# The tail of a two-layer backbone: wide products for output tiles 4 to 6, the last tile finished half by half

## Chip, cores and metric

The kernel runs on one core of a Trainium2 chip. The metric is device time of one execution in microseconds (us), median of several runs. The engines of the core are named as in the profile: PE (TensorE, products), DVE (VectorE), ACT (ScalarE), POOL (GpSimd) and SP (SyncE, which issues the transfers here). Each engine works through its own instructions strictly in the order in which they were placed, and waits for the others by semaphores.

## What is computed

A backbone of two layers over 1024 latent tokens and 256 context tokens with 1024 features: windowed attention, then a bidirectional state-space mixer (SSD), each with a gated residual, and a final normalisation. What matters here is the end of the second layer and the last line:

```python
def rms_normalize(x):
    xf = x.astype(jnp.float32)
    return (xf * lax.rsqrt(jnp.mean(xf * xf, axis=-1, keepdims=True) + EPS)).astype(x.dtype)

def back(y_f, y_b, xs, z):                      # end of the SSD mixer
    ...
    u = rms_normalize(u.reshape(bsz, n, SSD_GROUPS, SSD_WIDTH // SSD_GROUPS))
    return (u.reshape(bsz, n, SSD_WIDTH) * norm_w) @ w_out      # 2048 -> 1024

    h = h + gate[:, None] * y
return rms_normalize(h) * final_norm_w
```

So for each token: a product of 2048 features with `w_out` gives 1024 outputs, a gate and the residual `h` follow, and the token is scaled by the root of the mean of its 1024 squares and by a weight per output.

## The kernel before

**Layout.** Outputs lie on partitions: the 1024 outputs are eight tiles m = 0 to 7 of 128, tokens run along the free axis in two blocks, 0 to 511 and 512 to 1023. An fp32 product is made of three: features and weights are split into a high part in a rounded format (`oH`, `wh`) and the rest (`oL`, `wl`), and `mm3` (L223 to L225) sums high x high, low x high and high x low in one accumulator. For one output tile that is 16 feature tiles x 3 products.

**Stages of `ssd_out`.** Sweeps of products (L1571, 512 tokens wide, four output tiles at once, beside the last state-space work) finish all eight tiles of the first 512 tokens and tiles 0 to 3 of the second 512. Gates for these are the DVE operations of L1577. Then comes the tail, which the change rewrites:

- The first 512 tokens: `rstd_c` turns the sums of squares (`prev["acc"]`) into 1/root. PE sums over partitions (L344), ACT takes the root (L352), DVE the reciprocal (L353) and a diagonal matrix with it (L355), PE spreads that over all partitions (L357), ACT copies the result to SBUF (L359). `tail` then scales each of the eight tiles on DVE (L1479, one operation for weight and 1/root) and SP stores it (L1482). These tiles lie in the buffers named `uH` and `uL` in the profile.
- Tiles 4 to 7 of the second 512 tokens: each tile has two accumulators of 256 tokens in the two buffers `pj2`. For each of two steps (e = 0, 1: eight feature tiles each) it loads 512 KB of weights (L216, `wr`), ACT rounds them (L209, `wh`), DVE takes the rest (L211, `wl`), and PE runs 24 products for the first 256 tokens and 24 for the second (L223 to L225, 256 wide). There are two buffers each of `wr`, `wh` and `wl`. Then come the gates of both halves (L1611), and `final` adds their squares (ACT L1467 or L1470, POOL or DVE L1471).
- The second 512 tokens, after all products: `rstd_c` for each half of 256, and `tail` for pairs of tiles, six on DVE, tiles 3 and 7 (`TAILP`) with the 1/root on POOL (L1476) and the weight on ACT (L1477). One store per pair and half; the tiles lie in buffers named `xn`.

**What sets the order.** The code gives a program order; a scheduler then places the instructions of each engine by its own estimates of when they can start, keeping all dependencies. So the order on an engine can differ from the code, and it is fixed when the kernel is built.

Of the kernel before, what the change touches and what calls it, by code (L numbers as in the profile page):

```python
# [17 lines left out]
P = 128  # L18
D = 1024
KT = D // P  # L20
LAT = 1024
# [21 lines left out]
    pj=1, S=2, pt=2, pv=1,  # L43
# [8 lines left out]
PARTS = 8  # L52
SLACK = (0, 0, 0)
QC = 5
TAILP = (3, 7)
N512, N256 = 0.229, 0.120
FRONT = 4 * 48 * N512 + 3 * 24 * N256 + 8 * 24 * N256
OUT = 4 * 30 * 3 * N512
# [46 lines left out]
class Kernel:  # L105
# [1327 lines left out]
    def ssd_out(self, p, spare, sp, sc, post):  # L1433


        nc, t, a = self.nc, self.t, self.a
        ps = self.psA
        BUFS.update(oraw=4)
        fw = t(self.cp, [P, KT], F32, "fw")
        nc.sync.dma_start(fw, a["final_w"])  # L1440
        h, pair, prev = {}, {}, {}

        def weights(m, k0, k1):
            w = []
            for e in range(2):
                lo, hi = max(k0, 8 * e), min(k1, 8 * e + 8)
                if lo < hi:
                    wh, wl = self.load_w(a["w_so"][m, e][:, (lo - 8 * e) * P : (hi - 8 * e) * P], hi - lo)
                    w += [(wh[:, x], wl[:, x]) for x in range(hi - lo)]
            return w  # L1450

        def residual(m, s, n):
            i = s // 512
            if i == 0:
                if m % 4 == 0:
                    self.h4 = t(self.up, [P, 4, n], F32, ("uH2", "uL2")[m // 4])
                h[m] = self.h4[:, m % 4]
            else:
                if m % 2 == 0:
                    pair[m] = self.h4 = t(*spare[m // 2])  # L1460
                h[m] = self.h4[:, m % 2]
            nc.sync.dma_start(h[m], self.h_d[m][i][:, s - 512 * i : s - 512 * i + n])

        def square(m, s, n, hm, first, dve):
            if first:
                self.acc = t(*{0: (sp, [P, n], F32, "xn2"), 512: (sp, [P, n], F32, "bn2"), 768: (sc, [P, n], F32, "xs")}[s])
                nc.scalar.activation(self.acc, hm, AF.Square)  # L1467
            else:
                sq = t(sp, [P, 512], F32, "bn4")[:, :n]
                nc.scalar.activation(sq, hm, AF.Square)  # L1470
                (nc.vector if dve else nc.gpsimd).tensor_tensor(self.acc, self.acc, sq, op=ALU.add)  # L1471

        def tail(s, n, h, r, k, m0):
            for m in range(m0, m0 + k):
                if k > 1 and m in TAILP:
                    nc.gpsimd.tensor_tensor(h[m], h[m], r, op=ALU.mult)  # L1476
                    nc.scalar.activation(h[m], h[m], AF.Copy, scale=fw[:, m : m + 1])  # L1477
                else:
                    nc.vector.scalar_tensor_tensor(h[m], in0=h[m], scalar=fw[:, m : m + 1], in1=r, op0=ALU.mult, op1=ALU.mult)  # L1479
            src = h[m0] if k == 1 else pair[m0][:, :, s - 512 : s - 512 + n]  # L1480
            dst = a["out"][m0 * P : (m0 + k) * P, s : s + n]
            nc.sync.dma_start(dst if k == 1 else dst.rearrange("(a p) n -> p a n", p=P), src)  # L1482
# [58 lines left out]
        for n, (i, mg, qs) in enumerate(sweeps):  # L1541
            if n == 3:
                alloc(1, 1)
            pj = [t(ps, [P, 2, 512], F32, "pj2") for _ in range(2)]
# [5 lines left out]
            for q in qs:  # L1550
                w = ws[j]
# [4 lines left out]
                for z in range(2):  # L1556
                    k = 2 * q + z
# [26 lines left out]
        post.flush()  # L1584

        self.ptag = "psX"
        acc, hs = {}, {512: {}, 768: {}}

        def final(m, s):
            h[m] = hs[s][m] = pair[m - m % 2][:, m % 2, s - 512 : s - 256]  # L1590
            self.acc = acc.get(s)
            square(m, s, 256, h[m], m == 0, m == KT - 1)
            acc[s] = self.acc

        for m in range(4):
            for s in (512, 768):
                final(m, s)
        r = self.rstd_c(p, prev["acc"], 512, D, rout=(sc, [P, 512], F32, "y2"), dout=(sp, [P, 512], F32, "bn4"))
        for m in range(KT):
            tail(0, 512, prev["h"], r, 1, m)  # L1600
        for m in range(4, KT):
            residual(m, 512, 512)
            full = h[m]
            pj = {s: t(ps, [P, 512], F32, "pj2")[:, :256] for s in (512, 768)}
            for e in range(2):
                w = weights(m, 8 * e, 8 * e + 8)
                for s in (512, 768):
                    self.mm3(pj[s], [(*w[k], self.oH[e][:, k, s - 512 : s - 256], self.oL[e][:, k, s - 512 : s - 256]) for k in range(8)], e == 0, e == 1)
            for s in (512, 768):
                h[m] = full[:, s - 512 : s - 256]  # L1610
                nc.vector.scalar_tensor_tensor(h[m], in0=pj[s], scalar=self.mod[1][:, 16 + m, 0:1], in1=h[m], op0=ALU.mult, op1=ALU.add)  # L1611
                final(m, s)
        r = {s: self.rstd_c(p, acc[s], 256, D, rout=(sc, [P, 256], F32, x), dout=(sp, [P, 512], F32, "bn4")) for s, x in ((512, "y2"), (768, "hx"))}
        for m in range(0, KT, 2):
            for s in (512, 768):
                tail(s, 256, hs[s], r[s], 2, m)

    def dump_split(self, name, h, l, i, n, s):
        nc = self.nc
# [97 lines left out]
```

## Time and profile before

| | |
|---|---|
| median of 3 runs | 1819.51 us (1817.31 to 1822.76) |
| profiled execution, its own time | 1818.37 us |
| its span, first to last instruction | 1816.6 us |
| PE busy | 1749.0 us, 96% |
| DVE, ACT, POOL busy | 64%, 48%, 45% |
| mean granted PE clock | 0.99 |
| last product of the tail ends | about 1800.9 us |

Rows of a chain or a timeline give start, length, engine, what is written (`<-` what is read), line, and a count where several are merged. Buffer numbers are left out, so `pj` is any product accumulator, `psX` a small accumulator, `bn` a scratch tile. A bracket at the end of a row is the idle time of the engine before it, and what ended it.

### The profile page before, as it was taken

What the parts mean: (1) busy time and instruction counts of PE and PEld (TensorE: products, weight loads), DVE (VectorE), ACT (ScalarE), POOL (GpSimd) and SP (SyncE); (2) the same over time, 40 slices, a digit from 0 to 9 for tenths busy, and PEclk for the clock granted to TensorE, in tenths of its full rate; (3) what the DMA queues carried; (4) which work ended last, traced back from release to release, by engine and by line L of the source; (5) the groups of instructions that cost most, each with busy time, mean ns of one, the idle gap of its engine ahead of it and who ended that gap; (6) DMA issues with size and microseconds to landing.
All of it is one profiled execution on the core that took longest, in us unless ns stands there. A gap on an engine that the chain in (4) does not pass through costs nothing.

```text
span 1816.6 us, 29129 instructions
## 1 busy us (share of the span) xinstructions
PE 1749.0 (96%) x10379; PEld 1500.2 (83%) x10379; DVE 1166.0 (64%) x2125; ACT 869.9 (48%) x1895; POOL 811.1 (45%) x1074
## 2 busy tenths in 40 slices
PE   6999998999999899999999999999999999999997
PEld 3797767788889687778898898989889898988886
DVE  3563536786787766675766748567675857766643
ACT  3521235677788766352444434344353434544522
POOL 2441127554456465303454544646454454644311
PEclk9999999999999999999999999999999999999998
DMA  8768865543345445311322323323332322655542
GB/s 296 285 156 255 261 192 138 119 116 99 99 117 132 118 133 195 112 42 52 86 68 79 93 69 88 82 71 79 78 93 78 82 79 74 188 163 179 163 137 70
DMA packets 209393, 227.89 MB, mean 125 GB/s; under 512 B 16096, under 2 KB 149088, under 8 KB 208224
## 3 DMA queue, kind: packets, MB, share of 16 engines
q1 hardware_dynamic: 175184, 207.38, 38.1%
q0 software_dynamic: 34064, 18.65, 5.6%
q8 instruction: 82, 1.34, 0.3%
q14 instruction: 63, 0.52, 0.1%
HBM read 191.14 MB, written 35.13 MB: 125 GB/s over the span
## 4 chain that ended last, share of the span: by engine, by line
PE 83%; DVE 5%; ACT 4%; DMA 4%; issue 3%; POOL 0%; SPq 0%; DVEq 0%; ACTq 0%; POOLq 0%
PE pj L1152 17%; PE pj L1177 10%; PE pj L1571 7%; PE pj L223 6%; PE pj L225 6%; PE pj L224 6%; PE psD L1143 3%; PE pt L694 3%; PE psX L1311 2%; PE pv L701 2%; PE psD L1236 2%; PE pv L700 2%; PE S L669 2%; PE psX L1285 1%; PE S L670 1%
## 5 line engine op out<-in xcount | busy, mean ns | idle before, releaser
L223 PE MATMUL pj<-uH,wh 128*128 128x256 f32 (+1 forms) x652 | 233.5, 358 | 8.1 <-DVE rope_b L532 2.3
L224 PE MATMUL pj<-uL,wh 128*128 128x256 f32 (+1 forms) x652 | 220.1, 338 | 0.0
L225 PE MATMUL pj<-uH,wl 128*128 128x256 f32 (+1 forms) x652 | 220.1, 338 | 0.0
L211 POOL TENSOR_TENSOR wl<-wr,wh 128x512 fp32r<-128x512 f32 x92 | 121.7, 1326 | 97.4 <-ACT wh L209 96.9
L1152 PE MATMUL pj<-uH,wh 128*128 128x512 f32 x480 | 161.4, 410 | 2.0 <-ACT xn L1088 1.2
L1152 PE MATMUL pj<-uH,wl 128*128 128x512 f32 x480 | 158.5, 403 | 0.0
L1152 PE MATMUL pj<-uL,wh 128*128 128x512 f32 x480 | 157.3, 402 | 0.0
L699 DVE TENSOR_TENSOR pl<-pt,ph 128x512 fp32r<-128x512 f32 x168 | 114.2, 687 | 61.3 <-ACT ph L698 60.4
L223 PEld LDWEIGHTS pj<-uH,wh 128*128 128x128 f32 x652 | 124.7, 191 | 34.9 <-issue 8.6
L1177 PE MATMUL pj<-wh,uH 128*128 128x256 f32 x512 | 148.0, 289 | 3.1 <-ACT xn L1088 3.0
L1177 PE MATMUL pj<-wl,uH 128*128 128x256 f32 x512 | 150.7, 294 | 0.0
L1213 POOL TENSOR_TENSOR xw<-xn,dtdec 128x256 f32<-128x256 f32 x144 | 92.9, 649 | 127.1 <-PE psD L1236 108.5
L1177 PE MATMUL pj<-wh,uL 128*128 128x256 f32 x512 | 149.5, 292 | 0.0
L1342 ACT ACTIVATE uT<-psX,nw 128x128 f32<-128x128 f32 x128 | 46.7, 365 | 193.2 <-PE psX L1341 193.1
L225 PEld LDWEIGHTS pj<-uH,wl 128*128 128x128 f32 x652 | 124.4, 191 | 14.8 <-issue 1.7
L673 DVE CUSTOM_DVE_ANT_0 sm<-S,mask,nsink 128x640 f32<-128x640 f32 (+2 forms) x160 | 118.7, 772 | 26.5 <-PE S L670 14.5
L224 PEld LDWEIGHTS pj<-uL,wh 128*128 128x128 f32 x652 | 124.9, 192 | 11.5 <-issue 2.8
L209 ACT CAST wh<-wr 128x512 fp32r<-128x512 f32 (+1 forms) x132 | 84.8, 645 | 102.5 <-PE pj L224 78.7
L698 ACT CAST ph<-pt 128x512 fp32r<-128x512 f32 x168 | 97.5, 585 | 64.5 <-PE pt L694 58.9
L675 ACT ACTIVATE sm<-sm,nm 128x640 f32<-128x640 f32 (+2 forms) x160 | 118.5, 742 | 12.6 <-DVE nm L673 12.3
L1152 PEld LDWEIGHTS pj<-uL,wh 128*128 128x128 f32 x480 | 90.1, 188 | 19.0
L1152 PEld LDWEIGHTS pj<-uH,wh 128*128 128x128 f32 x480 | 89.1, 188 | 19.6 <-ACT bn L1088 2.0
(383 smaller groups left out, 4999.8 us busy)
## 6 DMA issues: line engine op xcount, KB each, us to landing
fd<-acs SPq DMA_DIRECT2D x64, 256.0 KB, 5.0
bd<-acs SPq DMA_DIRECT2D x64, 256.0 KB, 5.2
wr<-w_x SPq DMA_DIRECT2D x31, 512.0 KB, 3.8
wr<-w_sk SPq DMA_DIRECT2D x24, 512.0 KB, 4.0
wr<-wg SPq DMA_DIRECT2D x44, 256.0 KB, 4.6
qs<-q POOLq DMA_DIRECT2D x40, 256.0 KB, 3.9
wr<-wo SPq DMA_DIRECT2D x40, 256.0 KB, 2.7
wada<-w_ad SPq DMA_DIRECT2D x8, 1024.0 KB, 6.4
```

The lines of the kernel that those rows point to most:

```text
L211: (eng or nc.vector).tensor_tensor(l, raw, h, op=ALU.subtract)
L223: self.nc.tensor.matmul(ps, lh, rh, start=first and i == 0, stop=False)
L224: self.nc.tensor.matmul(ps, lh, rl, start=False, stop=False)
L225: self.nc.tensor.matmul(ps, ll, rh, start=False, stop=last and i == n - 1)
L673: nc.vector.tensor_tensor_reduce(out=sm[:, :W], in0=Sv, in1=self.mask[:, m0 : m0 + W], scale=-SCALE, scalar=self.nsink[:, 4 * j + r : 4 * ...
L675: nc.scalar.activation(sm[:, :W], sm[:, :W], AF.Exp, bias=nm[:, r : r + 1], scale=-1.0, accum_out=sums[:, r : r + 1])
L698: nc.scalar.copy(ph, ptf)
L699: nc.vector.tensor_sub(pl, ptf, ph)
L1152: nc.tensor.matmul(raw[:, 512 * i : 512 * i + 512], l[:, k, :], r[i][:, k, :], start=k + y == 0, stop=k == KT - 1 and y == 2)
L1177: nc.tensor.matmul(pj[:, c], l, r[:, k, :], start=c % 2 + q + k + y == 0, stop=c % 2 == 1 and q == 1 and k == 3 and y == 2)
L1213: nc.gpsimd.tensor_tensor(xw, X(st, c).rearrange("p (r h) -> p r h", r=R), self.dtdec[:, c, hd(d, g)].unsqueeze(2).broadcast_to([P, R, HP] ...
L1571: nc.tensor.matmul(banks[x], l[:, z, sl], r, start=k == 2 * qs[0] and y == 0, stop=k == 2 * qs[-1] + 1 and y == 2)
```

## The change

1. Tiles 4 to 6 of the second 512 tokens use one accumulator of 512 tokens and 512-wide products: 48 products a tile instead of 96.
2. Weights are asked for one step ahead in the code.
3. The last tile keeps two halves of 256 tokens with an accumulator each. Each half runs all its products, then its gate, its square and its own `finish`: row sums, root, reciprocal, diagonal, spread, scaling of all eight tiles, stores.
4. The weight of the last line is multiplied in ahead (`square_w` for tiles 0 to 6, one line in the loop for tile 7, on ACT), so that `finish` only multiplies by 1/root: tiles in pairs, three pairs on DVE, which reads the factor from PSUM (`pr`), tiles 2 and 3 on POOL, which reads the copy in SBUF (`r`).
5. In `tail`, which now serves the first 512 tokens alone, odd tiles go to POOL (factor) and ACT (weight), even ones stay on DVE. The calls stand between the steps of products instead of ahead of them.
6. Squares of the second 512 tokens are summed 512 wide on POOL, in a buffer `cT`; the last tile's squares are added by PE as a second product of the row sum.

```diff
-TAILP = (3, 7)
...
         def tail(s, n, h, r, k, m0):
             for m in range(m0, m0 + k):
-                if k > 1 and m in TAILP:
+                if m % 2:
                     nc.gpsimd.tensor_tensor(h[m], h[m], r, op=ALU.mult)
                     nc.scalar.activation(h[m], h[m], AF.Copy, scale=fw[:, m : m + 1])
                 else:
...
+        acc = t(sp, [P, LAT], F32, "cT")[:, :512]
+
+        def square_w(m):
+            if m == 0:
+                nc.scalar.activation(acc, h[m], AF.Square)
+            else:
+                sq = t(sp, [P, 512], F32, "bn4")
+                nc.scalar.activation(sq, h[m], AF.Square)
+                nc.gpsimd.tensor_tensor(acc, acc, sq, op=ALU.add)
+            nc.scalar.activation(h[m], h[m], AF.Copy, scale=fw[:, m : m + 1])
+
+        def gated(m, pj, sl):
+            nc.vector.scalar_tensor_tensor(h[m][:, sl], in0=pj, scalar=self.mod[1][:, 16 + m, 0:1], in1=h[m][:, sl], op0=ALU.mult, op1=ALU.add)
+
+        def finish(i, sq):
+            pn = t(ps, [P, 512], F32, "psX")
+            lo = 256 * i
+            for b in range(2):
+                for x, y in enumerate((acc[:, lo:], sq)):
+                    nc.tensor.matmul(pn[:, b : b + 1], y[:, b * P : (b + 1) * P], self.ones[:, 0:1], start=x == 0, stop=x == 1)
+            rc = t(p, [P, 4], F32, "rc", 2)[:, :2]
+            nc.scalar.activation(rc, pn[:, :2], AF.Sqrt, bias=self.eps, scale=1.0 / D)
+            nc.vector.reciprocal(rc, rc)
+            dg = t(sp, [P, 512], F32, "bn4")[:, :256].rearrange("p (b n) -> p b n", b=2)
+            nc.vector.tensor_tensor(dg, self.ident.unsqueeze(1).broadcast_to([P, 2, P]), rc.unsqueeze(2).broadcast_to([P, 2, P]), op=ALU.mult)
+            pr = t(ps, [P, 512], F32, "psX")[:, :256]
+            nc.tensor.matmul(pr, self.ones, dg.rearrange("p b n -> p (b n)"), start=True, stop=True)
+            r = t(sc, [P, 256], F32, ("y2", "hx")[i])
+            nc.scalar.copy(r, pr)
+            for m in (0, 2, 4, 6):
+                v = pair[m][:, :, lo : lo + 256]
+                eng, x = (nc.gpsimd, r) if m == 2 else (nc.vector, pr)
+                eng.tensor_tensor(v, v, x.unsqueeze(1).broadcast_to([P, 2, 256]), op=ALU.mult)
+                nc.sync.dma_start(a["out"][m * P : (m + 2) * P, 512 + lo : 768 + lo].rearrange("(a p) n -> p a n", p=P), v)
 
         for m in range(4):
-            for s in (512, 768):
-                final(m, s)
+            square_w(m)
+        w = weights(4, 0, 8)
         r = self.rstd_c(p, prev["acc"], 512, D, rout=(sc, [P, 512], F32, "y2"), dout=(sp, [P, 512], F32, "bn4"))
-        for m in range(KT):
-            tail(0, 512, prev["h"], r, 1, m)
-        for m in range(4, KT):
+        for m in range(4, KT - 1):
             residual(m, 512, 512)
...
-            pj = {s: t(ps, [P, 512], F32, "pj2")[:, :256] for s in (512, 768)}
+            pj = t(ps, [P, 512], F32, "pj2")
             for e in range(2):
...
+                cur, w = w, weights(m + e, 8 - 8 * e, 16 - 8 * e)
+                self.mm3(pj, [(*cur[k], self.oH[e][:, k, :], self.oL[e][:, k, :]) for k in range(8)], e == 0, e == 1)
+                tail(0, 512, prev["h"], r, 1, 2 * m - 8 + e)
+            gated(m, pj, slice(0, 512))
+            square_w(m)
+        m = KT - 1
+        residual(m, 512, 512)
+        ws7 = [w, weights(m, 8, 16)]
+        for x in (6, 7):
+            tail(0, 512, prev["h"], r, 1, x)
+        for i in range(2):
+            sl = slice(256 * i, 256 * i + 256)
+            pj = t(ps, [P, 512], F32, "pj2")[:, :256]
+            for e in range(2):
+                self.mm3(pj, [(*ws7[e][k], self.oH[e][:, k, sl], self.oL[e][:, k, sl]) for k in range(8)], e == 0, e == 1)
+            gated(m, pj, sl)
+            sq = t(sp, [P, 512], F32, "bn4")[:, :256]
+            nc.scalar.activation(sq, h[m][:, sl], AF.Square)
+            nc.scalar.activation(h[m][:, sl], h[m][:, sl], AF.Copy, scale=fw[:, m : m + 1])
+            finish(i, sq)
```

Up to the start of tile 4 the order of PE, DVE, POOL and SP is the same in both kernels, and ACT's up to the last squares of tiles 0 to 3. Line numbers in the changed kernel are one lower up to the tail (L1478 is the former L1479), and the gate is L1598.

On DVE, around the gate of tile 4 (the one that writes `xn` from an accumulator `pj`), this stands in a row before; `wl` is the rest of the weights of one step, and `uH`, `uL` are the scaled tiles of the first 512 tokens:

```order
L211 TENSOR_TENSOR wl_18684<-wr_18680,wh_18682 128x1024
L1479 SCALAR_TENSOR_TENSOR uH_3616_17227<-uH_3616_17227,fw_17207,y_3856_18539 128x512 x4
L1479 SCALAR_TENSOR_TENSOR uL_3720_17728<-uL_3720_17728,fw_17207,y_3856_18539 128x512 x4
L1611 SCALAR_TENSOR_TENSOR xn_3857_18557<-pj_3858_18559,mod_6_75,xn_3857_18557 128x256
L1611 SCALAR_TENSOR_TENSOR xn_3857_18557<-pj_3859_18560,mod_6_75,xn_3857_18557 128x256
L211 TENSOR_TENSOR wl_18738<-wr_18734,wh_18736 128x1024
```

And there now:

```order
L210 TENSOR_TENSOR wl_18579<-wr_18575,wh_18577 128x1024
L1478 SCALAR_TENSOR_TENSOR uH_3616_17227<-uH_3616_17227,fw_17207,y_3855_18538 128x512 x2
L1478 SCALAR_TENSOR_TENSOR uL_3720_17728<-uL_3720_17728,fw_17207,y_3855_18538 128x512 x2
L1598 SCALAR_TENSOR_TENSOR xn_3856_18540<-pj_3857_18542,mod_6_75,xn_3856_18540 128x512
L210 TENSOR_TENSOR wl_18619<-wr_18615,wh_18617 128x1024
```

Four scalings instead of eight stand ahead of the gate, and one gate of 512 takes the place of two of 256. The other four scalings are now POOL and ACT instructions.

On PE, the end of the last tile now; `psX` is the row sum of half 0, `cT` the squares of tiles 0 to 6, `bn` those of tile 7, and `pj_3892` the accumulator of half 1:

```order
L223 MATMUL pj_3892_18845<-uL_3805_18199,wh_18761 128x256
L1605 MATMUL psX_18823<-ones_68,bn_3886_18820 128x1
L1605 MATMUL psX_18823<-ones_68,cT_18505 128x1
L1605 MATMUL psX_18823<-ones_68,bn_3886_18820 128x1
L224 MATMUL pj_3892_18845<-uH_3804_18198,wl_18763 128x256
```

Before, all products of both halves stand ahead of the first row sum:

```order
L224 MATMUL pj_3890_18918<-uL_3805_18199,wh_18975 128x256
L225 MATMUL pj_3890_18918<-uH_3804_18198,wl_18977 128x256
L344 MATMUL psX_19035<-ones_68,bn_3844_18505 128x1 x2
L357 MATMUL psX_19043<-bn_3901_19041,ones_68 128x256
L344 MATMUL psX_19047<-ones_68,xs_18507 128x1 x2
```

Half 0's row sums now stand seven products ahead of the end of half 1, whose last 34 products all come after half 0's last.

On DVE after the last gate, where `psX_18833` is the spread factor of half 0 and `psX_18908` that of half 1:

```order
L1598 SCALAR_TENSOR_TENSOR xn_3873_18685<-pj_3892_18845,mod_6_75,xn_3873_18685 128x256
L1618 TENSOR_TENSOR xn_3808_18202<-xn_3808_18202,psX_18833 128x2x256
L1618 TENSOR_TENSOR xn_3856_18540<-xn_3856_18540,psX_18833 128x2x256
L1618 TENSOR_TENSOR xn_3873_18685<-xn_3873_18685,psX_18833 128x2x256
L1608 RECIPROCAL rc_18903<-rc_18903 128x2
L1610 TENSOR_TENSOR bn_3896_18906<-ident_63,rc_18903 128x256
L1618 TENSOR_TENSOR xn_3808_18202<-xn_3808_18202,psX_18908 128x2x256
```

Six narrow scalings per half have become three wide multiplies, and half 1's reciprocal stands behind those of half 0.

On SP, loads of weights (`wr`) and stores of the first 512 tokens (`out`), now:

```order
L215 DMA wr_18647<-w_so 128x1024
L1481 DMA out<-uH_3616_17227 128x512 x3
L1481 DMA out<-uL_3720_17728 128x512 x2
L1481 DMA out<-uH_3616_17227 128x512
L1481 DMA out<-uL_3720_17728 128x512
L215 DMA wr_18688<-w_so 128x1024
L1481 DMA out<-uL_3720_17728 128x512
L215 DMA wr_18720<-w_so 128x1024
```

The load for tile 6's second step (`wr_18688`) stands behind seven of the eight stores, three of which wait for POOL and ACT; before, it stood behind all eight, which waited for DVE alone.

More of the change, by code (lines that the diff above doesn't have):

```diff
@@ L1586, in ssd_out @@
         self.ptag = "psX"
[L1587 to L1593, printed above, removed]
+        acc = t(sp, [P, LAT], F32, "cT")[:, :512]
[7 more added lines that the diff above has]
+            nc.scalar.activation(h[m], h[m], AF.Copy, scale=fw[:, m : m + 1])
@@ L1605, in ssd_out @@
             for e in range(2):
[L1606 to L1616, printed above, removed]
+                cur, w = w, weights(m + e, 8 - 8 * e, 16 - 8 * e)
+                self.mm3(pj, [(*cur[k], self.oH[e][:, k, :], self.oL[e][:, k, :]) for k in range(8)], e == 0, e == 1)
+                tail(0, 512, prev["h"], r, 1, 2 * m - 8 + e)
```

1 line of the change is left out of this document (removed).

## Prediction

> **What bounds the kernel now.** The page first: TensorE (PE) is busy almost throughout, so only a place where PE waits, or where nothing is left for it, can give time.
>
> ```profile
> span 1816.6 us, 29129 instructions
> PE 1749.0 (96%) x10379; PEld 1500.2 (83%) x10379; DVE 1166.0 (64%) x2125; ACT 869.9 (48%) x1895; POOL 811.1 (45%) x1074
> ```
>
> The change touches only what comes after the last sweep of products, from about 1750 us on. So the second view is the busy time in five stretches of that tail (columns: stretch, its length, busy us of PE, weight loads, DVE, ACT and POOL, then granted clock, DMA share, GB/s).
>
> ```profile
> 1762.50:1764.70 2.20, 0.28 (x3) 0.12 (x2) 2.20 (x5) 1.19 (x2) 0.00 (x0) 1.00 1.03 393
> 1764.70:1768.40 3.70, 3.70 (x19) 3.70 (x20) 1.29 (x2) 0.67 (x2) 2.15 (x2) 0.54 0.97 329
> 1768.40:1774.00 5.60, 5.60 (x49) 5.60 (x49) 0.86 (x1) 1.05 (x1) 0.00 (x0) 1.00 0.12 50
> ...
> 1800.90:1816.60 15.70, 2.54 (x13) 1.66 (x11) 8.80 (x18) 3.67 (x9) 3.17 (x4) 0.66 0.39 134
> ```
>
> PE is lost in three places: a hole at 1762.7, 3.7 us at a granted clock of 0.54 after it, and 15.7 us at the end with hardly a product. Third view, the chain of waits across the hole (start, length, what), and PE's own row at its end:
>
> ```profile
> 1728.56 11.04 PE pj L1571 x48
> ...
> 1750.09 0.36 PE pj L223
> ...
> 1757.16 0.88 PE psX L357 x2
> 1758.06 0.60 ACT y L359
> 1758.68 2.74 DVE uH L1479 x4
> 1761.42 1.35 DVE uL L1479 x3
> ...
> 1763.99 0.49 DVE xn L1611
> ...
> 1764.61 0.36 PE pj L223
> ...
> 1768.50 0.12 PE pj L223
> ```
>
> ```profile
> 1764.61 0.36 PE L223 MATMUL pj<-uH,wh 128*128 128x256 f32 x1 [1.92 <-DVE xn L1611]
> ```
>
> DVE scales eight finished tiles of the first 512 tokens (L1479) in one run; the gate of output tile 4 (L1611) stands behind them, and tile 5 can't start, since both its accumulators are still held by tile 4. Fourth, the chain from the last product to the end, POOL's part of the first half's scaling, the first two store issues of the second half, and the bytes per second in 40 slices of 0.325 us from 1804:
>
> ```profile
> 1800.90 0.35 PE psX L344 x4
> ...
> 1801.28 0.27 ACT rc L352
> ...
> 1801.57 0.18 DVE rc L353
> ...
> 1801.77 0.44 DVE bn L355
> ...
> 1802.35 0.68 PE psX L357 x2
> ...
> 1803.46 2.70 DVE xn L1479 x4
> ...
> 1807.49 1.21 PE psX L357 x2
> ...
> 1808.73 0.38 ACT hx L359
> ...
> 1811.04 1.58 DVE xn L1479 x4
> ```
>
> ```profile
> 1803.50 1.58 POOL L1476 TENSOR_TENSOR xn<-xn,y 128x256 f32<-128x256 f32 x2 [11.25 <-ACT y L359]
> ```
>
> ```profile
> 1811.07 0.89 SPq L1482 DMA_DIRECT2D out<-xn  x2
> ```
>
> ```profile
> GB/s 0 0 0 0 0 0 0 280 331 347 321 356 328 359 331 353 221 0 0 0 0 0 0 0 148 328 359 315 372 318 359 347 350 315 16 0 0 0 0 0
> ```
>
> Both 256-token halves are finished one behind the other on DVE, after all products.
>
> **The sum, part by part.** Prices come from these groups (mean ns after the bar), besides the rows above:
>
> ```profile
> L1286 DVE TENSOR_TENSOR fd<-fd,psX 128x512 f32<-128x512 f32 x64 | 43.7, 683 | 25.6 <-ACT fd L1272 13.5 <-PE psX L1282 10.3 <-PE psX L1341 1.3
> L1471 POOL TENSOR_TENSOR xn<-xn,bn 128x512 f32<-128x512 f32 x7 | 11.1, 1589 | 9.4 <-ACT bn L1470 8.9
> L291 ACT ACTIVATE uH<-uL,mod 128x512 fp32r<-128x512 f32 x12 | 8.7, 723 | 10.3 <-DVE uL L290 10.2
> L211 DVE TENSOR_TENSOR wl<-wr,wh 128x1024 fp32r<-128x1024 f32 x8 | 9.8, 1222 | 18.3 <-ACT wh L209 18.3
> L209 ACT CAST wh<-wr 128x1024 fp32r<-128x1024 f32 x8 | 8.4, 1046 | 23.8 <-PE pj L224 16.3 <-issue 4.4 <-PE pj L1571 3.1
> wr<-w_so SPq DMA_DIRECT2D x7, 512.0 KB, 3.6
> ```
>
> 1. Wide products in tiles 4 to 6. A tile now takes 96 products of 0.12 us, 11.52; afterwards 48 wide ones, and the sweep row has 48 in 11.04. Three tiles: 3 x 0.48 = 1.44 us gained, all on PE's path.
>
> 2. The hole. A tile now holds one accumulator, so tile 5 starts in the other without tile 4's gate. DVE scales four tiles instead of eight ahead of that gate, and POOL and ACT the other four. The 1.92 us go. What is late next? The weights of tile 5's second step: their low part stands on DVE behind the gate. Tile 4 now ends near 1750.1 + 11.04 + 0.88 = 1762.0; four scalings from 1758.68 take 2.74 alone, and beside POOL up to 2.70/1.58 times that (the two rows of four at the end; POOL worked beside the first from 1803.50 to 1805.08), 4.7, to 1763.4. Gate and low part (0.75 + 1.22, estimates from the gate's half of 0.49 and L211) end near 1765.5; the second step wants them at 1762.0 + 5.52 + 0.46 = 1768.0. Slack 2.5 us, cost nothing.
>
> 3. The slow clock. 3.70 us at 0.54 are 3.70 x 0.46 = 1.70 us of lost products; it follows the hole and should go with it.
>
> [...]
>
> 4. Weights a step ahead. Both kernels have two buffers of each part, so the cast for step s+1 starts when PE has left step s-1, one step (5.52 us) ahead; cast and low part need 1.05 + 1.22 = 2.3. Nothing gained, nothing lost while ACT's other new work fits: per tile two casts (2.1), a square and a weight multiply (about 0.72 each, L291), in tile 4 four more multiplies (2.9): at most 6.5 of 11.04. On SP the load for tile 6's second step now stands behind seven stores, three of which wait for POOL and ACT: POOL's four multiplies by L1471's 1.59 run to about 1765.1, so the load lands before 1770 (3.6 us); it is wanted at 1773.1. Nothing.
>
> 5. The finish. Let E be the end of the last product. PE now takes half 0's row sums in seven products before E (7 x 0.12 = 0.84). From the rows above: root 0.27, reciprocal 0.18, diagonal 0.44 with gaps of 0.02 to 0.14 end at E + 0.23; spread 0.68, copy 0.38 (DVE's multiply waits for that copy) to E + 1.3; then three multiplies on DVE of 128x2x256, with the scale read from PSUM. No row shows this shape. Lower bound and value taken 0.683 (L1286: the same size, with a broadcast operand in PSUM); upper bound 1.35, two narrow L1479 as they ran beside POOL (2 x 2.70/4). To E + 3.4. Half 1's gate, square and sums are done by then; its reciprocal and diagonal stand behind those multiplies: E + 4.2, spread 1.21 (as after the long idle now; 0.68 at best), copy: E + 5.8. The first store follows a multiply later; SP then waits for POOL's multiply of tiles 2 and 3 (1.5 taken, a little under the two narrow ones' 1.58, since it is one instruction) and issues the last three from about E + 7.3. In the trace data starts 0.9 us after the issue at 1811.07 (slice 24, 1811.9), and four stores take ten slices, 0.8 each; the last slice ends at 1815.1, 1.5 before the end of the span. So E + 7.3 + 0.9 + 2.3 + 1.5 = E + 12.0, against 15.7 now (1800.90 to 1816.6): 3.7 gained. Bounds: 0.68 for the spread gives 4.2; 1.35 for the multiplies costs 2.0 for half 0 and about as much for half 1, and nothing of the 3.7 remains.
>
> [...]
>
> Sum: 1.44 + 1.92 + 1.70 + 3.7 = 8.8, less 0.35 for the row sums that now stand between products (the row at 1800.90): 8.4 us. The profiled execution took 1818.37 (1816.6 and 1.8 around it), 1.1 under the median 1819.51, to which I apply it: 1811.1. POOL's wider sums of squares (1.59 each) lie beside products: three from about 1752, before its first multiply can start at 1758.7, then one per tile.
>
> **Rivals.** Bound of "no change": 0.3%, 5.5 us, about what a measurement of this kernel can tell.
>
> 1. As summed: 1811.1; its own range 1808 (spread 0.68 and a low run, as 1817.31 is 2.2 under its median) to 1813.5.
>
> 2. The finish gains nothing: the new multiplies take 1.35. For it: the slow first four L1479 beside POOL. Against it: the PSUM operand of L1286 at 0.683 over 64 instances. 1811.1 + 4.0 = 1815.1, "no change".
>
> 3. POOL holds DVE in the middle. If scalings and POOL's multiplies exclude each other fully, DVE's fourth ends at 1758.7 + 4 x 0.69 + 3 x 1.59 = 1766.2, and the low part, past the gate and POOL's fourth, at about 1769.2 instead of 1768.0: a hole of 1.2, and 1.7 more if the clock falls again. 1811.1 + 2.9 = 1814.0. Against it: four L1479 beside two POOL multiplies took 2.70, less than 1.58 + 1.58. [...]
>
> 4. The slow clock belongs to the burst of stores (DMA share 0.97 to 1.03 in both rows), not to the hole. The same eight stores remain. 1811.1 + 1.7 = 1812.8.
>
> 5. Slower: the weight casts come late. If ACT has over 5.52 - 2.3 = 3.2 us of other work in front of each cast, every step waits for its weights: seven further steps x 2.4 = 16.8, less 8.4: 1827.9. Only tile 4 has so much ACT work, most of it in its first step, before the next cast is possible.
>
> **How the numbers follow.** Chances: 0.60, 0.14, 0.12, 0.09, 0.05 in that order. Faster by over 0.3% (under 1814.0): 1 but for a high run (0.58), 4 (0.09), half of 3 (0.06), a part of 2 (0.05): 0.78. Within 0.3%: the rest of 1, 2 and 3: 0.17. Slower: 5, 0.05. The range runs from 1807.0 (all lower bounds and a low run) to 1815.5, just past rival 2.
>
> **What would show it.** Right: tiles 4 to 7 of products without a gap from 1750.1 to about 1796.2 with the clock at 1.00; the scaling of the first 512 tokens ends on DVE before 1764; three DVE multiplies near 0.69 us each per half; about 12 us from the last product to the end. Wrong: a PE row waiting for the low part (wl) or the cast in tile 5 or 6 (rivals 3, 5); a clock near 0.5 without a hole (4); the multiplies above 1 us (2). The part before 1750 us should not move; if it does by more than 2 us, the sum is wrong for a reason I do not see.

## The result and the profile after

The changed kernel took 1805.28 us (median of 6 runs, 1804.25 to 1809.08), the kernel before 1817.06 beside it (6 runs, 1814.91 to 1822.76): ratio 0.9935, interval [0.9918, 0.9952], a gain of 11.8 us. The forecast was 1811.1 with a range from 1807.0. Two later loads of the same two kernels gave ratios of 0.9952 [0.9940, 0.9963] and 0.9956 [0.9944, 0.9968], gains of 8.7 and 8.0 us; over all runs the medians are 1809.08 (17 runs) and 1817.26 (66 runs), 8.2 us apart. So the change is worth about 8.2 us, close to the 8.4 of the sum; what the first comparison shows beyond that comes from the part of the kernel that the change does not touch, as shown below.

The page of after (span, busy time, granted clock in 40 slices):

```profile
span 1802.2 us, 28825 instructions
...
PE 1741.2 (97%) x10243; PEld 1488.7 (83%) x10243; DVE 1162.7 (65%) x2110; ACT 875.4 (49%) x1897; POOL 815.5 (45%) x1070
...
PEclk9999999999999999999999999999999999999998
```

The span is 14.4 us shorter. I cut it at the first of the four gates that end the last sweep (L1577 before, L1576 after: 1748.53 and 1742.35 us); what follows is called the tail. The tail went from 68.08 to 59.87 us, 8.2 shorter. The other 6.2 us lie ahead of it, where both kernels have the same instructions in the same order.

First the tail. Busy time from its first product to its last, and after it (columns as in the prediction):

```profile
1743.90:1790.40 46.50, 46.45 (x250) 39.75 (x250) 21.51 (x21) 19.29 (x28) 16.25 (x10) 1.00 0.31 102
...
1790.40:1802.20 11.80, 2.81 (x12) 1.93 (x12) 4.74 (x10) 1.74 (x5) 2.54 (x2) 0.61 0.52 178
```

PE is busy 46.45 of 46.50 us at a granted clock of 1.00; the hole and the 0.54 behind it are gone. What PE waits for in the tail (in all, times, longest) names neither a low part (wl) nor a gate. This view counts idle time only; a short delay between overlapping products does not show in it (point 2 below has one).

```profile
PE psX L1612 <- DVE bn L1610: 2.3, 2, 2.1
PE pj L222 <- ACT cT L1590: 0.2, 1, 0.2
```

The chain at the end (start, length, what):

```profile
1788.85 0.57 PE psX L1605 x6
...
1790.02 0.42 DVE bn L1610
...
1790.44 0.44 DVE xn L1598
...
1791.38 0.29 ACT y L1614
...
1791.70 1.88 DVE xn L1618 x3
1793.58 0.09 DVE rc L1608
...
1793.76 0.44 DVE bn L1610
...
1794.33 1.21 PE psX L1612 x2
...
1795.56 0.38 ACT hx L1614
...
1795.97 0.69 DVE xn L1618
```

The last product ends at 1790.35, just ahead of half 1's gate (L1598), and the span at 1802.22: 11.9 us, where before had 15.7.

Now the part ahead of the tail. Three stretches of it in before, in after, and in after loaded once more (e2_after below); the column behind the last bracket is the granted clock:

```profile
255.00:355.00 100.00, 88.45 (x444) 71.34 (x443) 66.28 (x182) 58.05 (x158) 62.74 (x90) 0.93 0.56 136
...
600.00:630.00 30.00, 24.48 (x128) 18.61 (x127) 21.66 (x47) 18.75 (x42) 10.07 (x16) 1.00 0.46 122
...
740.00:840.00 100.00, 93.21 (x495) 76.40 (x494) 66.40 (x92) 45.02 (x79) 17.64 (x23) 0.98 0.22 66
```

```profile
255.00:355.00 100.00, 88.31 (x479) 71.21 (x478) 71.69 (x193) 63.48 (x171) 66.04 (x95) 1.00 0.59 142
...
600.00:630.00 30.00, 25.81 (x126) 20.62 (x127) 21.42 (x46) 19.23 (x43) 11.54 (x18) 0.94 0.48 129
...
740.00:840.00 100.00, 93.21 (x513) 77.52 (x512) 65.75 (x91) 44.30 (x77) 12.41 (x22) 0.97 0.22 60
```

```profile
255.00:355.00 100.00, 88.20 (x443) 70.79 (x442) 66.75 (x179) 58.12 (x159) 63.36 (x91) 0.93 0.58 136
...
600.00:630.00 30.00, 24.46 (x129) 18.73 (x128) 22.50 (x49) 18.85 (x44) 10.07 (x16) 1.00 0.44 114
...
740.00:840.00 100.00, 93.20 (x477) 75.98 (x476) 65.30 (x91) 44.97 (x79) 16.23 (x21) 0.95 0.23 66
```

In the first stretch before was granted 0.93, after 1.00, and the same program loaded again 0.93. The granted clock falls to 0.5 in periods of 3.41 us. One that products fill costs about half its length, 1.7 us: the hole of 1.92 us in before's tail and the period behind it were worth 3.6 together (e5_gate_first). The record of the clock has 6 such periods ahead of before's tail, 4 ahead of after's and 8 ahead of after's second load.

The counts alone do not give the times: two periods are 3.4 of the 6.2 us. Matched product by product, after is 1.0 us ahead of before at 200 us, 6.4 at 400, 6.0 at 800 and 6.2 at the gate. So 5.4 us arise between 200 and 400 us, where before has four of its periods and after none, some 1.4 us for each. After's period at 605 us cost it nothing against before, which has none there.

### The profile page after: what moved, and what is told of

It is laid out like the page before. It is cut to its first block, busy times and chain, and to the rows that moved or that the text cites. A ratio compares the mean times of both kernels' runs of the same rounds, so it can differ in the third digit from the quotient of the medians.

```text
span 1802.2 us, 28825 instructions
## 1 busy us (share of the span) xinstructions
PE 1741.2 (97%) x10243; PEld 1488.7 (83%) x10243; DVE 1162.7 (65%) x2110; ACT 875.4 (49%) x1897; POOL 815.5 (45%) x1070
## 4 chain that ended last, share of the span: by engine, by line
PE 85%; DVE 6%; ACT 4%; DMA 3%; issue 2%; SPq 0%; POOL 0%; DVEq 0%; ACTq 0%; POOLq 0%
PE pj L1151 17%; PE pj L1176 10%; PE pj L1570 7%; PE pj L222 7%; PE pj L224 6%; PE pj L223 6%; PE psD L1142 3%; PE pt L693 3%; PE psX L1310 2%; PE pv L700 2%; PE psD L1235 2%; PE pv L699 2%; PE S L668 2%; PE psX L1284 1%; PE psX L1283 1%
## 5 line engine op out<-in xcount | busy, mean ns | idle before, releaser
L222 PE MATMUL pj<-uH,wh 128*128 128x512 f32 (+1 forms) x604 | 223.2, 370 | 6.7 <-DVE rope_b L531 2.3
L224 PE MATMUL pj<-uH,wl 128*128 128x512 f32 (+1 forms) x604 | 211.3, 350 | 0.0
L223 PE MATMUL pj<-uL,wh 128*128 128x512 f32 (+1 forms) x604 | 210.3, 348 | 0.0
L222 PEld LDWEIGHTS pj<-uH,wh 128*128 128x128 f32 x604 | 114.2, 189 | 35.2 <-issue 7.8
L224 PEld LDWEIGHTS pj<-uH,wl 128*128 128x128 f32 x604 | 114.0, 189 | 17.2 <-issue 1.9
L223 PEld LDWEIGHTS pj<-uL,wh 128*128 128x128 f32 x604 | 114.5, 190 | 13.1 <-issue 2.5
L674 ACT ACTIVATE sm<-sm,nm 128x640 f32<-128x640 f32 (+2 forms) x160 | 118.6, 742 | 12.2 <-DVE nm L672 11.9
L1151 PEld LDWEIGHTS pj<-uL,wh 128*128 128x128 f32 x480 | 90.1, 188 | 18.9
L1151 PEld LDWEIGHTS pj<-uH,wh 128*128 128x128 f32 x480 | 89.1, 188 | 19.6 <-ACT bn L1087 2.0
```

Source lines behind the costliest of these rows:

```text
L222: self.nc.tensor.matmul(ps, lh, rh, start=first and i == 0, stop=False)
L223: self.nc.tensor.matmul(ps, lh, rl, start=False, stop=False)
L224: self.nc.tensor.matmul(ps, ll, rh, start=False, stop=last and i == n - 1)
L674: nc.scalar.activation(sm[:, :W], sm[:, :W], AF.Exp, bias=nm[:, r : r + 1], scale=-1.0, accum_out=sums[:, r : r + 1])
L1151: nc.tensor.matmul(raw[:, 512 * i : 512 * i + 512], l[:, k, :], r[i][:, k, :], start=k + y == 0, stop=k == KT - 1 and y == 2)
```

## The experiments

For each profile: the time of the first gate, the half-clock periods ahead of it, and the tail. Up to the tail all of these programs have the same instructions in the same order. e1 to e4 ran on one chip (15), e5 to e8 on a second (12), e9 to e11 on a third (14); the chip of the first two profiles is not on record. e5 to e8 ran once each, so only their traces are read.

| profile | first gate, us | half-clock periods ahead | tail, us |
|---|---|---|---|
| before | 1748.53 | 6 | 68.08 |
| e1_before | 1747.72 | 6 | 68.06 |
| e11_before | 1746.06 | 6 | 68.06 |
| after | 1742.35 | 4 | 59.87 |
| e2_after | 1750.07 | 8 | 59.89 |
| e10_after | 1746.15 | 6 | 59.82 |
| e3_products | 1750.72 | 7 | 62.82 |
| e4_finish | 1747.48 | 6 | 63.53 |
| e5_gate_first | 1743.48 | 5 | 64.43 |
| e6_all_dve | 1745.89 | 6 | 59.64 |
| e7_sbuf | 1746.55 | 6 | 61.30 |
| e8_holes | 1744.68 | 4 | 111.25 |
| e9_order | 1745.06 | 5 | 58.98 |

The first gates lie at 1747.5 to 1750.7 us on the first of these chips, 1743.5 to 1746.6 on the second and 1745.1 to 1746.2 on the third. So the chip may have a part in the spread; no run separates it from the load. Profiles of one chip still differ by up to 3.2 us.

**e1_before, no edit.**

> The kernel before, once more. Theory A (chance ahead of the tail): the tail gained what was summed, and the rest of the 11.8 us lies in stretches whose instructions the change does not touch, where the clock falls to 0.5 for 3.4 us behind short holes of TensorE, or does not, from one execution to the next. Then this profile reaches the first gate of the tail (1748.5 us in the profile of before, 1742.35 in that of after) at a time of its own, between about 1741 and 1751, with a number of half-clock windows ahead of the tail other than the 6 of before, each worth 1.7 us; the tail itself, from that gate to the end of the span, lasts 68.1 us within 1, or 1.7 less if the hole at its middle is not followed by a slow clock. Time against itself: ratio 1.000 within 0.002. Theory B (the change makes the untouched part faster, by its place in memory or its fewer instructions): the gate comes at 1748.5 within 1 us again, with the same six windows.

The gate came at 1747.72, inside theory B's 1 us, with six periods again, but at other places (one near 269 us, two in a row near 337, one at 621, where the first profile had four between 263 and 345 and none at 621). Times: 1815.11 (11 runs) against 1818.14 (19 runs), ratio 0.9985 [0.9975, 0.9995]. By the gate this did not part the theories. It showed that two loads of one program on one chip can lie 3 us apart, outside an interval that counts runs as independent.

**e2_after, no edit.**

> The changed kernel, once more. Theory A: the first gate of the tail at a time of its own between about 1739 and 1749, the number of half-clock windows ahead of it other than 4; the tail 59.9 us within 0.7. The gain in the median over five rounds is that of the tail, 8.2 us (ratio 0.9955), within the 3 us or so by which single runs differ. Theory B: the gate at 1742.4 within 1 us again, and the gain 11 to 14 us again (ratio 0.993).

This parted them: gate at 1750.07, 7.7 us later than in the first profile of the same program, with 8 periods instead of 4. The tail is 59.89 (59.87). Time 1811.21, gain 8.7 us. Theory B, that the change makes the untouched part faster, falls: on the same chip before's gate came earlier (1747.72, e1_before), and on the third chip the two came together (1746.06 and 1746.15).

**e3_products, the products alone.** Tiles 4 to 6 as in after, without the weight multiply ahead; tile 7 and the finish as in before:

```diff
-            nc.scalar.activation(h[m], h[m], AF.Copy, scale=fw[:, m : m + 1])
...
+        pj = {s: t(ps, [P, 512], F32, "pj2")[:, :256] for s in (512, 768)}
+        for e in range(2):
+            for s in (512, 768):
+                self.mm3(pj[s], [...], e == 0, e == 1)
...
+        r = {s: self.rstd_c(p, acc[:, s - 512 : s - 256], 256, D, ...) for s, x in ((512, "y2"), (768, "hx"))}
+        for m in range(0, KT, 2):
+            for s in (512, 768):
+                tail(s, 256, hs[s], r[s], 2, m)
```

> The product part alone: wide products in tiles 4 to 6, weights a step ahead, odd tiles of the first 512 tokens on POOL and ACT, but the finish of before (all eight tiles scaled with the final weight after the last product, half by half). By the terms of the prediction (1.44 for the wide products, 1.92 for the hole, 1.70 for the slow clock) the tail lasts 68.1 - 5.1 = 63.0 us, the time is 5.1 below before (ratio 0.9972). If the gain of the change lay in the finish alone: 68 us. If this stretch gained more than summed (7 or more), the tail is under 61.

Tail 62.82, 5.2 shorter (5.1 expected); ratio 0.9970 [0.9957, 0.9983], 5.4 us.

**e4_finish, the finish alone.** Products and scalings as in before, then after's tile 7 and finish:

```diff
-        w = weights(4, 0, 8)
...
+        for m in range(KT):
+            tail(0, 512, prev["h"], r, 1, m)
+        for m in range(4, KT - 1):
+            residual(m, 512, 512)
+            pj = {s: t(ps, [P, 512], F32, "pj2")[:, :256] for s in (512, 768)}
...
+            for s in (512, 768):
+                gated(m, pj[s], slice(s - 512, s - 256))
+            square_w(m)
```

> The finish alone: the last tile in two halves, each finished by itself, the final weight multiplied in ahead; tiles 4 to 6 as narrow products with two accumulators each, and all eight scalings of the first 512 tokens on DVE ahead of tile 4's gate, as before. By the prediction's terms 3.7 less 0.35: the tail lasts 68.1 - 3.3 = 64.8 us, with the hole of 1.9 us still there (64.8 with a slow clock behind it, 63.1 without); ratio 0.998. If the finish gained nothing: 68.

Tail 63.53; 63.1 was expected without a slow clock behind the hole. The hole is there:

```profile
PE pj L222 <- DVE xn L1598: 1.7, 1, 1.7
```

Here is the period of the clock that holds it and the next one, in before and in e4_finish (the first number behind the comma is PE's busy time):

```profile
1761.50:1764.91 3.41, 1.49 (x12) 1.31 (x12) 3.41 (x7) 1.40 (x2) 0.00 (x0) 1.00 1.03 392
1764.91:1768.33 3.42, 3.42 (x18) 3.42 (x17) 1.08 (x1) 0.46 (x2) 2.15 (x2) 0.51 0.97 328
```

```profile
1760.62:1764.03 3.41, 1.68 (x14) 1.50 (x13) 3.41 (x6) 1.36 (x2) 0.00 (x0) 1.00 0.77 286
1764.03:1767.45 3.42, 3.42 (x31) 3.42 (x30) 0.72 (x1) 1.04 (x2) 1.43 (x1) 1.00 1.02 305
```

PE idle for 1.92 us in the one, clock 0.51 next; idle for 1.73 in the other, clock 1.00 next. The second rows have the burst of stores alike (DMA share 0.97 and 1.02), so the stores do not lower the clock by themselves. Without the 1.7 us of slow clock the finish brought 68.07 - 1.70 - 63.53 = 2.8 us (3.3 expected); the 5.2 of e3_products and these 2.8 make 8.0 of the 8.2. In time the kernel was 8.4 us faster, ratio 0.9954 [0.9941, 0.9967], though its tail gained 4.5: its five runs had a mean granted clock of 0.9930, the runs of before 0.9894.

**e5_gate_first, the hole alone.** In before, the scalings are put behind the gates, `g` being the last gate of tile m:

```diff
-        for m in range(KT):
-            tail(0, 512, prev["h"], r, 1, m)
...
+            with self.tc.issue_after(g.ins):
+                for x in range(3 * (m - 4), min(3 * (m - 3), KT)):
+                    tail(0, 512, h0, r0, 1, x)
```

> The kernel before with one thing moved: the eight scalings of the first 512 tokens stand on DVE behind the gates of tiles 4, 5 and 6 (three, three, two) instead of ahead of tile 4's gate. Narrow products and the finish stay. By the prediction's points 2 and 3 the hole of 1.92 us and the 1.7 us of slow clock behind it go: the tail (first gate to end of span) lasts 68.07 - 3.62 = 64.5 us; the hole alone, if the clock had not fallen: 66.1. If the wait only moves to tile 5's second step (its low part now stands behind three scalings): 67 or more. The gate that opens the tail comes at a time of its own (1742 to 1751).

Tail 64.43, 3.6 shorter, as expected. PE's one wait in the product stream is the first:

```profile
PE pj L223 <- ACT xs L1467: 0.2, 1, 0.2
```

So hole and slow clock were worth 3.6 us together; the 5.2 of e3_products leave 1.6 for the wide products.

**e6_all_dve, no help from POOL and ACT for the first 512 tokens.**

```diff
-                if m % 2:
+                if k > 1:
                     nc.gpsimd.tensor_tensor(h[m], h[m], r, op=ALU.mult)
```

> The changed kernel with all eight scalings of the first 512 tokens on DVE and none on POOL and ACT. In the profile of after, four of them took 7.0 us on DVE beside POOL's four multiplies (6.45 us). If DVE and POOL exclude each other there, eight on DVE alone take 8 x 0.69 = 5.5 us, less than four now, and tile 4's gate comes 1.5 us earlier; nothing else moves, since neither was on the path: tail 59.9 us within 0.5. If the division of the scalings was what removed the hole, DVE is now late: four more scalings of 1.75 each are 7 us, and a hole of several us opens in tile 5: tail 62 or more.

Tail 59.64 (59.87). The scalings in after on DVE and POOL, then in e6_all_dve on DVE alone (shortest, median, longest ns):

```profile
L1478 DVE SCALAR_TENSOR_TENSOR uH<-uH,fw,y x2: 1782/1834/1885, 1752.9 to 1754.7; 128x512 f32<-128x512 f32 x2
L1478 DVE SCALAR_TENSOR_TENSOR uL<-uL,fw,y x2: 1781/1782/1783, 1756.4 to 1758.1; 128x512 f32<-128x512 f32 x2
...
L1475 POOL TENSOR_TENSOR uL<-uL,y x2: 1744/1746/1747, 1755.9 to 1757.6; 128x512 f32<-128x512 f32 x2
```

```profile
L1478 DVE SCALAR_TENSOR_TENSOR uH<-uH,fw,y x4: 747/748/754, 1756.5 to 1758.5; 128x512 f32<-128x512 f32 x4
```

Eight scalings alone take 8 x 0.747 = 6.0 us, less than four beside POOL (7.0). Handing half of this work to POOL made DVE later, not earlier; the hole closed by the second accumulator, not by the division. On DVE alone the low part behind tile 4's gate ends 17.80 us after the first gate, against 19.36 in after, 1.6 earlier (1.5 expected).

**e7_sbuf, the factor of the finish from SBUF.**

```diff
-                eng, x = (nc.gpsimd, r) if m == 2 else (nc.vector, pr)
+                eng, x = (nc.gpsimd if m == 2 else nc.vector, r)
```

> The changed kernel with the multiplies of the finish reading their factor from SBUF (the copy that POOL reads) instead of PSUM on DVE. If the PSUM operand is what lets DVE work beside POOL (three multiplies of 0.63 us each beside one of 1.27 us on POOL), DVE now waits for POOL or POOL for DVE: the three multiplies of a half take 1.88 + 1.27 = 3.1 us, and the tail about 1.3 us longer (61.2) if half 1's stores are moved by it. If the operand's place does not matter: 1.9 us and 59.9.

Tail 61.30, 1.4 longer, as expected if DVE and POOL exclude each other. DVE's multiplies in after, and half 1's in e7_sbuf:

```profile
L1618 DVE TENSOR_TENSOR xn<-xn,psX x6: 680/682/689, 1791.7 to 1797.2; 128x512 f32<-128x512 f32 x6
```

```profile
L1618 DVE TENSOR_TENSOR xn<-xn,hx x3: 678/691/1751, 1801.2 to 1803.5; 128x512 f32<-128x512 f32 x3
L1618 POOL TENSOR_TENSOR xn<-xn,hx x1: 1767/1767/1767, 1801.3 to 1801.3; 128x512 f32<-128x512 f32 x1
```

With the factor in PSUM each takes 0.68 beside POOL's 1.27; with two operands in SBUF the one that starts beside POOL takes 1.75, and POOL's 1.77.

**e8_holes, twelve holes in the tail.** Behind every fourth group of three products of tiles 4 to 6 in after:

```diff
+        def hole(w, e, n):
+            pa, x = t(ps, [P, 512], F32, "psX"), t(sp, [P, 256], F32, "bn2")
+            with self.tc.issue_after(self.mm):
+                pre = nc.tensor.matmul(pa[:, :256], w[0][0], self.oH[e][:, 0, :256], start=True, stop=True)
+            nc.scalar.copy(x, pa[:, :256])
+            for _ in range(n):
+                nc.scalar.copy(x, x)
+            with self.tc.issue_after(pre.ins):
+                self.hole = nc.tensor.matmul(pa[:, 256:257], x[:, :P], self.ones[:, 0:1], start=True, stop=True).ins
...
+                    if k % 4 == 3:
+                        hole(cur, e, 3)
```

> The changed kernel with twelve holes of about 2 us put into TensorE's products of tiles 4 to 6, two in each step of 24 products: a small product, four copies of 128x256 in a row on ACT, and a product that reads the last of them, between two products. In all traces so far the half-clock stretches start on one grid of 3.413 us, and a stretch follows when TensorE was idle for more than about 1.8 us within one period of that grid (the same stall ahead of the tail is followed in one execution and not in another, as it falls on the grid). By this, of holes of 2 us about half (those with 1.8 us or more inside one period) are followed by a half clock in the next period, the others are not, and the period's idle time tells which. If a hole of this length is always followed, as the prediction took it: twelve of twelve. [...]

Ten of the twelve opened, most of them 1.82 to 4.0 us long; the last two were filled with other products. Periods of the clock's grid around three of the four holes of 1.82 us, and around one of 2.64 us (1790.2 to 1792.8):

```profile
1768.18:1771.59 3.41, 1.58 (x8) 1.14 (x8) 0.00 (x0) 1.58 (x4) 0.00 (x0) 1.00 0.00 0
1771.59:1775.01 3.42, 3.42 (x9) 2.69 (x9) 0.00 (x0) 0.00 (x0) 0.00 (x0) 0.50 0.00 0
...
1785.25:1788.66 3.41, 1.86 (x9) 1.59 (x10) 0.00 (x0) 1.40 (x4) 0.00 (x0) 1.00 0.02 5
1788.66:1792.07 3.41, 1.51 (x8) 0.99 (x6) 0.46 (x1) 1.78 (x4) 0.00 (x0) 1.00 0.00 0
1792.07:1795.49 3.42, 2.68 (x13) 2.25 (x14) 0.76 (x1) 0.65 (x2) 0.00 (x0) 1.00 0.37 120
...
1812.55:1815.97 3.42, 1.60 (x9) 1.34 (x9) 0.00 (x0) 1.58 (x4) 0.00 (x0) 1.00 0.00 0
1815.97:1819.38 3.41, 3.25 (x9) 2.16 (x7) 0.00 (x0) 0.06 (x1) 0.00 (x0) 0.50 0.00 0
```

The holes of 1.82 us that lie inside one period (at 1768.6, 1796.2 and 1812.6) were each followed by a period at 0.50. The one from 1785.0 to 1786.8 lies across a border, leaves 1.54 us of idle time in its period, and was not; nor was the longer hole of 2.64 us, which is cut into 1.87 and 0.74. Of nine periods at full clock with 1.8 us or more of idle time, eight were followed by a slow one, the ninth being the one with 1.90 in the row at 1788.66; of those with less, none. So "every hole of 2 us" does not hold, and 1.82 us can be enough. The idle time within a period of the grid fits, at about 1.8 us; why the one period escaped is open. The untouched part of all thirteen profiles agrees: of its full-clock periods after the first 60 us, all 26 with 1.8 us or more of idle time were followed by a slow one, 21 of the 73 with 1.35 to 1.8, and none with less. What parts the 21 from the 52 is open. Around the last product of the tail, periods with as little as 0.3 us of idle time by the profile (e2_after) were followed too, so there no such bound is shown.

**e9_order, a shorter finish.** Half 0's last two multiplies go behind half 1's diagonal:

```diff
-            nc.vector.tensor_tensor(dg, ...)
+            diag = nc.vector.tensor_tensor(dg, ...)
+            with self.tc.issue_after(diag.ins):
+                for f in rest:
+                    f()
...
-            for m in (0, 2, 4, 6):
+            for m in (0, 2) if i == 0 else (0, 2, 4, 6):
+                scale(m)
+            rest.extend([lambda: scale(4), lambda: scale(6)])
```

> The changed kernel with one order changed in the finish: DVE takes half 1's reciprocal and diagonal directly behind half 0's first multiply, and half 0's other two multiplies after them. In the profile of after, half 1's root was ready on ACT at 1792.56, but its reciprocal started at 1793.50, behind half 0's three multiplies; so half 1's spread, copy and multiplies come 0.9 us earlier, and the tail lasts 59.9 - 0.9 = 59.0 us. If the stores are the limit of the end instead (half 0's last two are now later): 59.9 or more. In the time of whole runs such a difference cannot be told from after (ratio against before as e10_after, within 0.002).

Its chain from half 1's root on:

```profile
1795.02 0.27 ACT rc L1607
...
1795.31 0.18 DVE rc L1608
...
1796.15 1.21 PE psX L1615 x2
...
1797.79 0.69 DVE xn L1621
```

The reciprocal follows the root at once, and the tail is 58.98 us, 0.9 under after's. Time 1807.92, ratio 0.9946 [0.9933, 0.9959], beside 0.9956 [0.9944, 0.9968] for after: it beats before, and after in the trace alone.

**e10_after and e11_before, a third load of each.**

> The changed kernel a third time, for the size of the gain. If the first result (11.8 us) held more than the tail's 8.2 us because of the half-clock stretches ahead of it, the gain over these rounds lies near 8.2, between 6 and 11, and span times granted clock (which takes the slow stretches out) differs from before by 5 to 6.5 us: the 8.2 less 1.7 for the slow stretch behind the hole and less what the slow stretch at the very end differs by. If the change itself makes the untouched part faster: 11 to 14 us again, and span times clock differs by 9 or more.

> The kernel before a third time, against itself on the same chip: how far two loads of the same program lie apart. In the first such pair it was 3.0 us in the medians (ratio 0.9985). If loads differ by chance, a ratio between 0.998 and 1.002 of either sign; the tail again 68.1 us, or 66.4 if the hole at its middle falls across the border of two periods of the 3.413 us grid, and span times clock equal to before's within 1 us.

Gain 8.0 us, tails 59.82 and 68.06; e11_before against before 0.9998 [0.9988, 1.0009]. Mean span times mean granted clock of each load, which takes the slow periods out: 1790.4, 1791.3 and 1790.9 for after, 1796.3 to 1797.0 for four groups of before. The difference of 5.8 us is about what the tail's 8.2 leaves without the 1.7 behind the hole and some 0.7 at the very end, where the half clock fills the last 10.6 to 10.9 us of the span in before's three profiles and 9.2 to 10.0 in after's. The measure is a rough one: for e4_finish it gives 1796.6, no gain, where its tail leaves 2.1 us by the same deductions. The size of the gain rests on the tails.

## Why the prediction was wrong

The sum came out nearly right (8.2 measured, 8.4 forecast), though one of its terms did not; the number it was taken from and the range around it were wrong. The step that failed is the one on the base: "1.1 under the median 1819.51, to which I apply it", with "as 1817.31 is 2.2 under its median" as the whole allowance for a low run, and with "The part before 1750 us should not move". That part moved by 6.2 us, and not because the sum was wrong, as the prediction would have read it, but because the part differs from load to load.

- The base. Three runs gave 1819.51; all 66 runs of that program give 1817.26. That is 2.3 us of the miss.
- The part ahead of the tail. It moved by 6.2 us between the two profiles, and by 7.7 between two loads of the same program. The six first runs of after had a mean granted clock of 0.9925, the next loads 0.9906 and 0.9905: 0.0019 to 0.002 of 1804 us, about 3.5 us. 1811.1 - 2.3 - 3.5 is the 1805.3 measured; the change does not explain that the first load of after was so quick, since two later loads were not. The profile of before showed it ahead of the result: a granted clock of 0.93 from 255 to 355 us, behind periods with 1.4 to 2.0 us of idle time. Had I counted those six periods at 1.7 us each as something that comes and goes, the range would have reached 3.4 us (two periods) further down. Why one load gets four and another eight is open.
- Points 1 to 3. Forecast 1.44 + 1.92 + 1.70 = 5.06; the products alone gained 5.2, the hole with its slow clock 3.6 (3.62), the wide products by difference 1.6 (1.44), with the delay of the next point in it. In all three profiles of before the hole fell 1.1 to 1.2 us behind a border of the grid, so its slow clock was regular.
- Point 2's cover was mis-sized. Four scalings beside POOL were put at 4.7 us and took 7.0. By rival 3 they would end at 1766.2; they ended at 1759.92, which in before's time is 1766.1. Its hole did not come: the low part stood behind the gate but not behind POOL's fourth multiply, and was ready at 1761.71 (1767.9 there, wanted at 1768.0). It was just too late all the same, as PE's first product with it shows:

```profile
1759.84 0.74 DVE L1598 SCALAR_TENSOR_TENSOR xn<-pj,mod,xn 128x512 f32<-128x512 f32 x1
1760.50 1.21 DVE L210 TENSOR_TENSOR wl<-wr,wh 128x1024 fp32r<-128x1024 f32 x1
...
1761.44 0.39 PE L223 MATMUL pj<-uL,wh 128*128 128x512 f32 x1
1761.77 0.50 PE L224 MATMUL pj<-uH,wl 128*128 128x512 f32 x1
```

  The two products start 0.33 us apart, the next two 0.34, where those around them start 0.22 to 0.24 apart. So the slack of 2.5 us was used up and 0.2 us lost; e6_all_dve has no such delay, and its tail is 0.2 us shorter. Rival 3 was right that DVE and POOL hold each other up (a scaling took 1.78 us beside POOL, 0.747 alone in e6_all_dve) and counted only one instruction too many.
- Half 0's row sums between products were put at 0.35 us. From the first gate to the end of the last product the tail takes 52.37 us in before, 48.73 without the hole (e5_gate_first), 47.13 with the wide products too (e3_products) and 48.00 in after: the row sums cost 0.87. Most of it stands between these two products, which start 0.71 us apart and not 0.12; the first pair of small products, at 1785.24, costs about 0.2 more:

```profile
1788.57 0.28 PE L223 MATMUL pj<-uL,wh 128*128 128x256 f32 x1
...
1789.28 0.36 PE L224 MATMUL pj<-uH,wl 128*128 128x256 f32 x1
```

  So e4_finish fell 0.5 short of its 3.3. The total of 8.2 came near 8.4 because points 1 and 5 gave a little more than forecast, which is luck.
- Point 4, weights a step ahead, cost nothing: PE waited for no cast and no load.
- Point 5. Forecast E + 12.0 (its three stores at 0.8 are 2.4, not the 2.3 of the sum), measured E + 11.9: 3.8 gained. The multiplies took 0.682 (0.683 taken), the spread 1.21 (1.21), POOL's multiply 1.27 (1.5). Rival 2's slow multiplies did not come; with the factor in SBUF one of three took 1.75 (e7_sbuf).
- Rival 4, the burst of stores, is out by e4_finish (DMA share 1.02 at a clock of 1.00) and after (clock 1.00 from 1743.90 to 1790.40); rival 5, late casts, did not occur.

## What to carry to other kernels

Cut two traces at the last instruction that a change cannot touch, and compare the parts on either side by themselves before explaining a difference of whole times: here the tail repeated within 0.1 us while the part ahead of it moved by 8. Stalls of TensorE can cost more than their length: here 47 of the 99 periods with 1.35 us or more of idle time were followed by 3.41 us at half clock; count them in the profile as an uncertainty of the time, and load both programs more than once, on the same chip, before a gain of less than 0.5% is sized. Before work is handed from DVE to POOL, see where the operands lie: with two of them in SBUF the two engines held each other up here, and DVE alone was quicker (eight scalings in 6.0 us, against four in 7.0 beside POOL).

## What the runs showed of the hardware

- All half-clock stretches of an execution start on one grid of 3.413 us: in the clock records of before and after each change of the clock lies within 0.003 us of it. In a dense stream of products 1.82 us of idle time inside one period were enough for a slow one, three times of three (e8_holes, rows at 1768.18 and 1812.55 and the hole at 1796.2). Ahead of the tail, where TensorE's work is sparser, 21 of 73 periods with 1.35 to 1.8 us of idle time were followed by a slow one, all 26 with more, and none with less.
- DVE with two SBUF operands and POOL reading SBUF held each other up: a scaling of 128x512 took 1.78 us beside POOL (after) and 0.747 alone (e6_all_dve). A multiply took 1.75 beside POOL with its factor in SBUF (e7_sbuf) and 0.68 with it in PSUM (after), POOL's beside it 1.77 and 1.27.
- Loads of one program differ in the granted clock: by 0.0012 on one chip (e1_before and before beside it, 3.0 us in the medians), by 0.002 between the first load of after and the later ones, perhaps on other chips. That is more than the 95% interval of a comparison of 5 to 19 runs allows for.
